# Weights of a macaron block laid out tile by tile by the host, with larger loads and retuned block numbers

## The chip, the core and the metric

The kernel runs on one core of a Trainium2 chip. TensorE (PE) multiplies, VectorE (DVE) and ScalarE (ACT) work element by element, GpSimd (POOL) does small things, and SyncE (SP) issues most DMA transfers. The metric is the device time of one execution in microseconds (us); given is the median of the runs.

## The reference

One transformer block for 256 tokens of width 2048, in float32: a SwiGLU FFN (hidden width 5632), a mixer (an RWKV-7 scan beside a pooling branch), and a second FFN, each with norms around it.

```python
def _swiglu(x, w_gate, w_up, w_down):
    return (jax.nn.silu(x @ w_gate) * (x @ w_up)) @ w_down

def _hybrid_mixer(u, w_in, ...):
    p = u @ w_in
    z_a, z_b, g_a, g_b = jnp.split(p, IN_SPLITS, axis=-1)
    y_a = _rwkv7_branch(z_a, ...) @ w_proj_a
    y_b = _pool_branch(z_b, pool_w, pool_scale) @ w_proj_b
    m = jax.nn.sigmoid(g_a) * y_a + jax.nn.sigmoid(g_b) * y_b
    return m @ w_out
...
        f = _swiglu(_rmsnorm(h, ln_ffn1_pre[l]), ffn1_gate[l], ffn1_up[l], ffn1_down[l])
        h = h + MACARON_WEIGHT * _rmsnorm(f, ln_ffn1_post[l])
        mx = _hybrid_mixer(_rmsnorm(h, ln_mix_pre[l]), ...)
        h = h + _rmsnorm(mx, ln_mix_post[l])
        f = _swiglu(_rmsnorm(h, ln_ffn2_pre[l]), ffn2_gate[l], ffn2_up[l], ffn2_down[l])
        h = h + MACARON_WEIGHT * _rmsnorm(f, ln_ffn2_post[l])
```

## The kernel before

**Products.** The 256 tokens are two row halves (h = 0, 1) of 128. A weight matrix is cut into tiles of 128 rows (index k) by 512 columns. Every float32 value is kept as a high and a low half: ACT casts a loaded weight (w) to its high half (wH), DVE subtracts it and leaves the low half (wL); the activations have xH and xL. One product is one row half times one tile, three matmuls of 512 columns (`mm3`: high x high, high x low, low x high). Weight tiles come two at a time (1024 columns wide) by `get_w` into one of 5 buffers w and are split into one of 5 pairs wH, wL. All these loads are issued on SP. In the old layout a load reads rows of 512 floats, 2 KB, out of the matrix as it is given.

**Quads.** For a pair of k tiles and two column blocks f and l (gate and up in the gate/up part, two column blocks of the down or output weights) there are 2 x 2 x 2 = 8 products. A quad does them in 7, with sums of weight tiles and sums of activation tiles. `raw4` loads its four weight tiles (into va and vb), DVE makes the sums (t13, then a sum written into w, then t4), and `halves` splits them. In the gate/up part a quad is done in two pieces: `early` (4 products), in the block before its own, and `late` (3 products, with the other two tiles loaded again by its own load) in its own block. `quad` does all seven at once in the down part and in the mixer's output.

**Order of the gate/up part.** There are 11 blocks of 512 gate columns and 512 up columns, each 16 k tiles deep. GATE1 and GATE2 give the number of quads of each block in the first and the second FFN. `block_seq` lays out a block's pieces: plain pairs of the gate, the late parts of its own quads between them, plain pairs of the up weights, and, spread over all of these, the early parts of the next block's quads. After each block DVE transposes the activations, and they go out to DRAM and back (cx, x).

**Parts' begins and ends.** The first product set of the first FFN (`head`) takes tokens from x_t, loaded a k tile or two at a time between the weights (xT), and k tiles one after the other. In the mixer and the second FFN the first set goes through `by_half`: the first LEAD k tiles are multiplied with row half 0, then with row half 1, so that row half 1 may be normalized later. There, the tiles from number STAG on get halves in buffers of their own (kH, kL, out of 34 units "u"). The same function does the last TRAIL tiles of a part's down product.

**Who sets the order.** The code records every operation (`Plan.add`), and a planner (`simulate`) works out an order for each engine with a list scheduler: it has a price for each operation (`cost`; for a DMA, bytes by a rate), a due time (`deadlines`), and a count of free buffers, and among ready operations it takes the one that is due first. The matmuls keep their program order within three streams: the scan chain first, then transposes ("side"), then the rest ("main"). `can` refuses an operation whose buffer isn't free; its rule on units keeps the last one for the scan chain. The result is emitted by one loop, so that all operations have the line L494 in the profile, and tiles are told apart by name. `set(behind=..., lag=...)` sets an operation's predecessor or due time; in `head` the sum of squares for the first norm (xq, px) starts behind k tile 11. `normed` forms the normalized activations (nx) and their sums (sf) for the quads.

## Time and profile before

| what | before |
|---|---|
| median of 3 runs | 2003.32 us (2002.46 to 2004.37) |
| the profiled execution | 2001.42 us, its span 1999.6 us |
| PE busy | 1988.3 us |
| DVE busy | 1782.8 us |
| ACT busy | 1179.8 us |
| loads issued on SP: bytes of that queue, share of the 16 DMA engines' time | 466.11 MB, 73.9% |

The span is the time from the first to the last instruction of the profiled execution. An engine's share says how much of it the engine was busy; a stage is read from its own stretch of the time. "[0.57 <-DVE wL]" behind a row means that the engine was idle for 0.57 us before it and that DVE's write of wL ended that. "512.0 KB, 4.7" in a row on transfers is the size of one and the median us from issue to landing. Names drop their numbers: f and l are the two column blocks' sums in PSUM, mm those of plain sets, p the extra sums of a quad, hH and hL the halves of t4.

### The profile page before, as it was taken

To read this page: it belongs to the slowest core of one execution; us is meant where nothing else is said; L and a number is where in the kernel's file an instruction comes from. 1 tells how busy PE (TensorE), PEld (TensorE's weight loads), DVE (VectorE), ACT (ScalarE), POOL (GpSimd) and SP (SyncE) were. 2 spreads that over 40 slices of the span, in tenths; PEclk is the share of its full clock that TensorE was granted. 3 is DMA by queue.
4 is the path that set the end of the run, shared out by engine and by line. 5 is a ranking of instruction groups with operands and counts; after the bars stand their busy time and mean duration, and the time that the engine had idled before them with its cause. 6 is when DMAs were issued, how large, how long until landed. Compare 5 with 4: busy or idle time off the path is not lost.

```text
span 1999.6 us, 28096 instructions
## 1 busy us (share of the span) xinstructions
PE 1988.3 (99%) x9751; PEld 1641.3 (82%) x9751; DVE 1782.8 (89%) x2320; ACT 1179.8 (59%) x1557; POOL 75.4 (4%) x142
## 2 busy tenths in 40 slices
PE   9999999999999999999999999999999999999998
PEld 7888888888888888888888788888888888788886
DVE  8989999999989867898859879898999999998896
ACT  7555556566555656864646445575555655655563
POOL 0000000000000020002200100010000000000000
PEclk9999999999999999999999999999999999999999
DMA  8788888887667787767576567777888888976674
GB/s 282 237 261 267 279 264 283 267 283 229 219 197 255 235 261 233 216 194 244 151 218 183 177 202 228 259 233 244 266 278 262 272 282 274 281 225 212 200 253 147
DMA packets 263198, 477.47 MB, mean 239 GB/s; under 512 B 22928, under 2 KB 50832, under 8 KB 263056
## 3 DMA queue, kind: packets, MB, share of 16 engines
q1 hardware_dynamic: 259536, 466.11, 73.9%
q0 software_dynamic: 3232, 9.44, 1.4%
q8 instruction: 76, 1.25, 0.2%
q14 instruction: 66, 0.54, 0.1%
q10 hardware_dynamic: 288, 0.14, 0.0%
HBM read 447.94 MB, written 26.61 MB: 237 GB/s over the span
## 4 chain that ended last, share of the span: by engine, by line
PE 66%; DVE 15%; DMA 9%; issue 7%; ACT 2%; SPq 1%; POOL 0%; DVEq 0%; ACTq 0%; POOLq 0%
PE mm L494 25%; PE l L494 17%; PE f L494 15%; DVE wL L494 7%; DMA w<-in_ffn_gate_dram 6%; PE p L494 5%; DVE t L494 3%; DMA w<-in_ffn_up_dram 2%; ACT wH L494 2%; DVE w L494 1%; SPq L494 1%; DMA x<-cx 1%; DVE sg L494 1%; DVE hL L494 1%; DVE f L494 1%
## 5 line engine op out<-in xcount | busy, mean ns | idle before, releaser
L494 ACT CAST wH<-w 128x1024 fp32r<-128x1024 f32 (+2 forms) x720 | 745.3, 1043 | 627.7 <-PE mm L494 155.6
L494 DVE TENSOR_TENSOR wL<-w,wH 128x1024 fp32r<-128x1024 f32 (+2 forms) x720 | 860.0, 1206 | 135.0 <-ACT wH L494 130.7
L494 PE MATMUL l<-wL,xH 128*128 128x512 f32 x770 | 300.0, 390 | 0.0
L494 PE MATMUL l<-wH,xL 128*128 128x512 f32 x770 | 299.6, 389 | 0.0
L494 PE MATMUL l<-wH,xH 128*128 128x512 f32 x770 | 299.6, 389 | 0.0
L494 PE MATMUL mm<-wL,xH 128*128 128x512 f32 (+1 forms) x656 | 254.6, 388 | 1.1 <-DVE wL L494 1.0
L494 PE MATMUL mm<-wH,xH 128*128 128x512 f32 (+1 forms) x656 | 254.3, 388 | 0.3 <-ACT xH L494 0.3
L494 PE MATMUL mm<-wH,xL 128*128 128x512 f32 (+1 forms) x656 | 253.8, 387 | 0.0
L494 PE MATMUL f<-wL,xH 128*128 128x512 f32 x644 | 251.0, 390 | 0.4 <-DVE wL L494 0.3
L494 PE MATMUL f<-wH,xH 128*128 128x512 f32 x644 | 250.7, 389 | 0.0
L494 PE MATMUL f<-wH,xL 128*128 128x512 f32 x644 | 250.5, 389 | 0.0
L494 DVE TENSOR_TENSOR t<-w,w 128x1024 f32<-128x1024 f32 (+1 forms) x166 | 168.9, 1017 | 18.4 <-DMA w<-in_ffn_gate_dram 14.1
L494 PEld LDWEIGHTS l<-wL,xH 128*128 128x128 f32 x770 | 144.5, 188 | 31.5 <-DVE wL L494 1.5
L494 PEld LDWEIGHTS l<-wH,xL 128*128 128x128 f32 x770 | 144.6, 188 | 29.8
L494 PEld LDWEIGHTS l<-wH,xH 128*128 128x128 f32 x770 | 144.6, 188 | 29.8
L494 PEld LDWEIGHTS mm<-wL,xH 128*128 128x128 f32 x656 | 123.2, 188 | 26.4 <-DVE wL L494 2.4
L494 PEld LDWEIGHTS mm<-wH,xH 128*128 128x128 f32 x656 | 123.2, 188 | 25.1 <-ACT xH L494 0.7
L494 PEld LDWEIGHTS mm<-wH,xL 128*128 128x128 f32 x656 | 123.2, 188 | 24.3 <-DVE xL L494 0.2
L494 PEld LDWEIGHTS f<-wL,xH 128*128 128x128 f32 x644 | 120.9, 188 | 26.6 <-DVE wL L494 1.7
L494 PEld LDWEIGHTS f<-wH,xL 128*128 128x128 f32 x644 | 120.9, 188 | 25.2
L494 PEld LDWEIGHTS f<-wH,xH 128*128 128x128 f32 x644 | 120.9, 188 | 24.9
L494 DVE TENSOR_TENSOR wL<-t,wH 128x1024 fp32r<-128x1024 f32 x103 | 125.2, 1216 | 3.9 <-ACT wH L494 3.6
(310 smaller groups left out, 2778.8 us busy)
## 6 DMA issues: line engine op xcount, KB each, us to landing
w<-in_w_in_dram SPq DMA_DIRECT2D x128, 512.0 KB, 4.5
w<-in_ffn_up_dram SPq DMA_DIRECT2D x113, 512.0 KB, 4.7
w<-in_ffn_gate_dram SPq DMA_DIRECT2D x109, 512.0 KB, 4.8
w<-in_ffn_down_dram SPq DMA_DIRECT2D x104, 512.0 KB, 4.5
w<-in_ffn_gate_dram SPq DMA_DIRECT2D x197, 256.0 KB, 4.2
w<-in_ffn_up_dram SPq DMA_DIRECT2D x189, 256.0 KB, 4.2
w<-in_ffn_down_dram SPq DMA_DIRECT2D x144, 256.0 KB, 3.9
cx<-T SPq DMA_DIRECT2D x32, 512.0 KB, 3.6
```

What stands on the lines that cost most here:

```text
L494: ins = o.fn(*[real(x) for x in o.a], **{n: real(x) for n, x in o.k.items()})
```

## The change

The host lays the large weights out. For gate with up, for down and for w_out (`Pairs`), the four tiles of a k pair and of the two column blocks stand side by side, 2048 floats a partition: plain pairs as f0, f1, l0, l1; quads as l0, f1, l1, f0, so that va and vb are each one piece of 4 KB a partition and the late part's two tiles (f1, l1) another. For w_in and the two projections (`Blocks`) a k pair of a column block is one piece of 1024 floats a partition. The narrow w_l and pool_w (`Rows`) and the tokens x_t stand k tile beside k tile, one long row a partition. `get_w` and `raw4` read these pieces; a quad's first part has two loads instead of four, a late part one instead of two.

The tokens of the first part are loaded at k = 1, 2, 4, 8 and 12, in pieces of 1, 2, 4, 4 and 4 k tiles. LEAD is 16 and STAG 6: at a part's begin all 16 k tiles go by row halves, and those from number 6 on have units of their own. GATE1 and GATE2 change at two and one places. In `ffn` the gate's activations are recorded ahead of the up product set and the squares' end (`finish`: px and the root) after the gate's. The planner's price of a load follows the longer runs (RATE), CARRY is longer, and a second rule on units (SPARE2) holds back operations of the scan chain that lie ahead of its next matmul while four or fewer units are free.

On SP at the kernel's start the loads stand so in the kernel before (w are weights, xT tokens):

```order
L494 DMA w_37_133<-in_ffn_gate_dram 128x512
L494 DMA xT_131<-in_x_t_dram 128x256
L494 DMA w_38_144<-in_ffn_gate_dram 128x512
L494 DMA xT_131<-in_x_t_dram 128x256
L494 DMA w_39_153<-in_ffn_gate_dram 128x512
L494 DMA xT_131<-in_x_t_dram 128x256
L494 DMA w_40_160<-in_ffn_gate_dram 128x512
L494 DMA xT_162<-in_x_t_dram 128x256
L494 DMA w_41_166<-in_ffn_gate_dram 128x512
```

and so in the changed one:

```order
L552 DMA w_37_133<-in_gate_up_dram 128x512
L552 DMA xT_131<-in_x_t_dram 128x256
L552 DMA w_38_144<-in_gate_up_dram 128x512
L552 DMA xT_131<-in_x_t_dram 128x512
L552 DMA w_39_153<-in_gate_up_dram 128x512
L552 DMA w_40_158<-in_gate_up_dram 128x512
L552 DMA xT_161<-in_x_t_dram 128x1024
L552 DMA w_41_163<-in_gate_up_dram 128x512
```

The tokens of k tiles 4 to 7 (128x1024) now stand ahead of the weight tile of k = 4.

On DVE, where the gate's product set of the first FFN ends and the up weights begin (wL_406 of before and wL_357 after are the first low half of the up weights, nx and xq the norm's adds), before:

```order
L494 TENSOR_TENSOR wL_361<-w_48_265,wH_352 128x1024
L494 TENSOR_TENSOR nx_370<-xH_168,xL_176 128x1024
L494 TENSOR_TENSOR xq_363<-xq_363,xq_372 128x1024
L494 TENSOR_TENSOR nx_389<-xH_215,xL_227 128x1024
L494 TENSOR_TENSOR xq_378<-xq_378,xq_385 128x1024
L494 TENSOR_TENSOR wL_406<-w_84_276,wH_393 128x1024
```

and after:

```order
L552 TENSOR_TENSOR wL_350<-w_48_237,wH_338 128x1024
L552 TENSOR_TENSOR wL_357<-w_84_247,wH_348 128x1024
L552 TENSOR_TENSOR nx_368<-xH_169,xL_178 128x1024
L552 TENSOR_TENSOR wL_379<-w_87_257,wH_359 128x1024
L552 TENSOR_TENSOR xq_366<-xq_366,xq_376 128x1024
L552 TENSOR_TENSOR nx_398<-xH_222,xL_227 128x1024
```

The first low half of the up weights moved from behind four adds to ahead of them.

On SP, where the first quad of the first FFN is loaded (w_161 and w_162 are its va and vb, cx the activations of block 0 on their way to DRAM), before:

```order
L494 DMA w_158_605<-in_ffn_gate_dram 128x2x512
L494 DMA w_161_626<-in_ffn_up_dram 128x512
L494 DMA w_161_626<-in_ffn_gate_dram 128x512
L494 DMA cx_87<-T_108_635 128x1024
L494 DMA w_162_655<-in_ffn_gate_dram 128x512
L494 DMA w_162_655<-in_ffn_up_dram 128x512
```

and after:

```order
L552 DMA w_158_591<-in_gate_up_dram 128x1024
L552 DMA cx_87<-T_108_620 128x1024
L552 DMA w_161_641<-in_gate_up_dram 128x1024
L552 DMA w_162_649<-in_gate_up_dram 128x1024
```

Four loads became two, and the store to cx stands ahead of both.

The diff, cut to its core:

```diff
@@ -36,8 +36,8 @@
-STAG = 8
-LEAD = 12
+STAG = 6
+LEAD = 16
@@ -47,13 +47,14 @@
-GATE1 = [0, 0, 2, 4, 3, 4, 3, 4, 3, 4, 4]
-GATE2 = [0, 0, 3, 4, 3, 4, 3, 4, 3, 4, 4]
+GATE1 = [0, 0, 2, 4, 3, 4, 3, 4, 3, 4, 3]
+GATE2 = [0, 0, 4, 4, 3, 4, 3, 4, 3, 4, 3]
+SPARE2 = 4
@@ -65,7 +66,60 @@
+XLOADS = {1: 1, 2: 2, 4: 4, 8: 4, 12: 4}
+SQLAG = 4000.0
+def down_quads(plan):
+    return [[2 * i for i in range(nq)] for nq, _, _ in plan]
+class Pairs:
+    def __init__(s, ap, KT, where):
+        s.ap, s.KT, s.where = ap, KT, where
+    def row(s, r):
+        return s.ap[r * P:r * P + P]
+    def get(s, j, n, c0, cw):
+        b, side = s.where(c0 // 512)
+        o = side * 1024 + j % 2 * 512
+        return s.row(b * s.KT // 2 + j // 2)[:, o:o + n * 512]
+    def quad(s, k, c0):
+        return s.row(s.where(c0 // 512)[0] * s.KT // 2 + k // 2)
+class Blocks:
+    def __init__(s, ap, KT, cols):
+        s.ap, s.KT, s.cols = ap, KT, cols
+    def get(s, j, n, c0, cw):
+        r = s.cols.index(c0) * s.KT // 2 + j // 2
+        return s.ap[r * P:r * P + P, j % 2 * 512:j % 2 * 512 + n * 512]
+class Rows:
+    def __init__(s, ap):
+        s.ap = ap
+    def get(s, j, n, c0, cw):
+        return s.ap[:, j * cw:(j + n) * cw]
+IN_COLS = ([z * W + h * 512 for z in range(3) for h in range(2)]
+           + [RCOLS + b * 512 for b in range(2)]
+           + [g + c * 512 for g in (GA, GB) for c in range(4)])
+ALL_COLS = [c * 512 for c in range(4)]
@@ -89,9 +143,10 @@
+RATE = 410.0
-CARRY = 1800.0
+CARRY = 2000.0
@@ -219,9 +274,8 @@
-            run = min(min(y.shape[-1] for y in w + r) * 4, 2048)
-            o.dur = o.nbytes / (387.0 if run >= 2048 else 387.0 * max(run, 64) * 1.25
-                                / (run + 512))
+            run = min(min(y.shape[-1] for y in w + r) * 4, 4096)
+            o.dur = o.nbytes / min(RATE, 484.0 * max(run, 64) / (run + 512))
@@ -320,9 +374,13 @@
-                if i.tag == "u" and o.stream != "chain" and len(slots["u"]) <= SPARE:
+                if i.tag == "u" and len(slots["u"]) <= max(SPARE, SPARE2):
-                    if q and q[0].nom <= o.nom < q[0].nom + HOLD:
+                    few = len(slots["u"]) <= SPARE
+                    if q and o.stream != "chain" and few and q[0].nom <= o.nom < q[0].nom + HOLD:
+                        return False
+                    if q and o.stream == "chain" and len(slots["u"]) <= SPARE2 \
+                            and o.nom > q[0].nom:
@@ -580,9 +638,7 @@
-        s.nc.sync.dma_start(out=w32[:, :n * cw].rearrange("p (k c) -> p k c", k=n),
-                            in_=w[j * P:(j + n) * P, c0:c0 + cw]
-                            .rearrange("(k p) c -> p k c", p=P))
+        s.nc.sync.dma_start(out=w32[:, :n * cw], in_=w.get(j, n, c0, cw))
@@ -711,8 +767,8 @@
         k = 0
         first(load, None, None)
         while k < KT:
-            if k:
-                first(load, k, n(k))
+            if k in XLOADS:
+                first(load, k, XLOADS[k])
             first(get, k, n(k))
             k += n(k)
         for k in range(4):
@@ -802,12 +858,11 @@
         s.nc.scalar.activation(out=s.rtmp("junk").bitcast(mybir.dt.bfloat16), in_=src,
                                func=AF.Square, accum_out=acc)
 
-    def raw4(s, k, wf, cf, wl, cl):
-        va, vb = [s.raw().rearrange("p (a c) -> p a c", a=2) for _ in range(2)]
-        for dst, kk, w, c0 in ((va[:, 0], k, wl, cl), (vb[:, 0], k, wf, cf),
-                               (va[:, 1], k + 1, wf, cf), (vb[:, 1], k + 1, wl, cl)):
-            s.nc.sync.dma_start(out=dst, in_=w[kk * P:kk * P + P, c0:c0 + 512])
-        return va, vb
+    def raw4(s, k, w, c0):
+        v = [s.raw() for _ in range(2)]
+        for i in range(2):
+            s.nc.sync.dma_start(out=v[i], in_=w.quad(k, c0)[:, i * 1024:i * 1024 + 1024])
+        return [t.rearrange("p (a c) -> p a c", a=2) for t in v]
 
     def halves(s, v, tag=None):
         m = v.shape[1]
@@ -874,10 +929,9 @@
-        vc = q.raw().rearrange("p (a c) -> p a c", a=2)
-        for i, (w, c0) in enumerate(((s.wf, s.cf), (s.wl, s.cl))):
-            q.nc.sync.dma_start(out=vc[:, i], in_=w[k * P + P:k * P + 2 * P, c0:c0 + 512])
-        b22, b21 = q.halves(vc)
+        vc = q.raw()
+        q.nc.sync.dma_start(out=vc, in_=s.wf.quad(k, s.cf)[:, 512:1536])
+        b22, b21 = q.halves(vc.rearrange("p (a c) -> p a c", a=2))
@@ -898,16 +952,16 @@
-        va, vb = q.raw4(k, s.wf, s.cf, s.wl, s.cl)
+        va, vb = q.raw4(k, s.wf, s.cf)
-        V.tensor_tensor(out=t13, in0=va, in1=vb[:, :1].to_broadcast([P, 2, 512]),
+        V.tensor_tensor(out=t13, in0=va, in1=vb[:, 1:].to_broadcast([P, 2, 512]),
-        V.tensor_tensor(out=vb[:, 0], in0=va[:, 0], in1=t13[:, 1], op=ALU.add)
+        V.tensor_tensor(out=vb[:, 1], in0=va[:, 0], in1=t13[:, 1], op=ALU.add)
-        V.tensor_tensor(out=t4, in0=vb[:, 1], in1=vb[:, 0], op=ALU.subtract)
+        V.tensor_tensor(out=t4, in0=vb[:, 0], in1=vb[:, 1], op=ALU.subtract)
-        t2, b21 = q.halves(vb)
+        b21, t2 = q.halves(vb)
@@ -1000,9 +1054,13 @@
         pss = [], []
 
         def hold(i):
-            return lambda h, ps: (pss[i].append(ps), h and ev("fl"[i], pss[i]))
+            return lambda h, ps: pss[i].append(ps)
         s.gemm_tok(wg, 0, at, NKD, hold(0), lead=True, xs=xs)
+        if xs:
+            xs[3]()
+        ev("f", pss[0])
         s.gemm_tok(wu, 0, at, NKD, hold(1))
+        ev("l", pss[1])
         rb = s.rtmp("rsb")
         s.spread(rs, rb)
         su = []
@@ -1874,15 +1936,15 @@
-                nc.scalar.dma_start(out=xT[0][:, :1], in_=x_t[:P].unsqueeze(1))
+                nc.scalar.dma_start(out=xT[0][:, 0], in_=x_t[:, :S])
-                out=xT[k // 4][:, k % 4:k % 4 + n],
-                in_=x_t[k * P:(k + n) * P].rearrange("(k p) t -> p k t", p=P))
+                out=xT[k // 4].rearrange("p k t -> p (k t)")[:, k % 4 * S:(k % 4 + n) * S],
+                in_=x_t[:, k * S:(k + n) * S])
...
+    def pairs(blocks, quads):
+        out = []
+        for (f, l), q in zip(blocks, quads):
+            kt = len(f)
+            v = _np.empty((kt // 2, P, 4, 512), _np.float32)
+            for i in range(kt // 2):
+                f0, f1, l0, l1 = f[2 * i], f[2 * i + 1], l[2 * i], l[2 * i + 1]
+                for m, t in enumerate((l0, f1, l1, f0) if 2 * i in q else (f0, f1, l0, l1)):
+                    v[i, :, m] = t
+            out.append(v.reshape(-1, 4 * 512))
+        return _np.concatenate(out)
+    def blocks(a, cols):
+        return _np.concatenate([tiles(a, c).reshape(-1, 2, P, 512).transpose(0, 2, 1, 3)
+                                .reshape(-1, 1024) for c in cols])
...
```

More of the change, by code (lines that the diff above doesn't have):

```diff
@@ L729, in head @@
                 s.late = last
-                with s.set(behind=last, lag=4000.0):
+                with s.set(behind=last, lag=SQLAG):
                     square()
@@ L1050, in down @@
     def down(s, wd, at, KT, ev, hT, sm, plan):
[L1051 to L1053 removed]
+        for c, (nq, first, step), ks in zip((0, 2), plan, down_quads(plan)):
+            J = Columns(s, wd, c * 512, wd, c * 512 + 512, at, KT, sm, ks, s.bank, s.psum)
             quads = list(J.quads)
@@ L1892, in turn @@
                                            op0=ALU.mult, op1=ALU.subtract)
+        sq = []
         def squares():
@@ L1966, in laid_out @@
         o += n * P
-    return (("x_t", _np.ascontiguousarray(_np.asarray(inputs["x"])[0].T)),
-            ("cols", _np.ascontiguousarray(cols.reshape(NCOL, P).T)))
+    return (("x_t", _np.ascontiguousarray(rows(_np.asarray(inputs["x"])[0].T, 0, S))),
+            ("cols", _np.ascontiguousarray(cols.reshape(NCOL, P).T)),
+            *((n, _np.ascontiguousarray(v, _np.float32)) for n, v in big))
 def kernel(**inputs):
```

74 lines of the change are left out of this document (50 added, 24 removed).

## The prediction

> **What bounds the kernel now.** I read the page first, then the stretches of the span by engine, then the waits of TensorE (PE) alone, and last the places in time where PE stops.
>
> ```profile
> span 1999.6 us, 28096 instructions
> PE 1988.3 (99%) x9751; PEld 1641.3 (82%) x9751; DVE 1782.8 (89%) x2320; ACT 1179.8 (59%) x1557; POOL 75.4 (4%) x142
> ```
> ```profile
> 150.00:420.00 270.00, 270.00 (x1192) 223.28 (x1190) 254.93 (x285) 160.45 (x195) 0.00 (x0) 1.00 0.85 273
> 740.00:900.00 160.00, 159.73 (x858) 135.71 (x857) 135.09 (x243) 108.08 (x181) 6.91 (x9) 1.00 0.72 217
> 900.00:1210.00 310.00, 309.81 (x2188) 252.82 (x2187) 253.10 (x443) 164.00 (x235) 35.77 (x57) 1.00 0.66 198
> 1300.00:1345.00 45.00, 45.00 (x209) 37.25 (x209) 44.10 (x79) 34.31 (x69) 8.36 (x10) 1.00 0.75 231
> ```
> ```profile
> PE po L494 <- ACT dg L494: 2.1, 1, 2.1
> ...
> PE mm L494 <- DVE wL L494: 1.0, 2, 0.6
> PE f L494 <- DVE wL L494: 0.9, 3, 0.6
> ```
> The columns of the stretches are length, then busy time (and count) of PE, weight load, DVE, ACT and POOL, granted clock, DMA share, GB/s. PE is busy throughout at the full clock, with 1192 matmuls in 270.00 us, so one matmul of 512 columns costs 0.2265 us and one product (three of them) 0.68 us. Its waits on weights add up to 1.9 us, and one wait of 2.1 us is in the last output. So what a faster DMA can buy directly is small. DVE is next: 254.93 of 270 us in the gate/up stretch, with DMA at 0.85. The real price of each stop is read from start to start:
>
> ```profile
> 17.01 0.39 PE L494 MATMUL mm<-wH,xH 128*128 128x512 f32 x1
> 17.97 0.50 PE L494 MATMUL mm<-wL,xH 128*128 128x512 f32 x1 [0.57 <-DVE wL L494]
> ...
> 28.75 0.39 PE L494 MATMUL mm<-wH,xH 128*128 128x512 f32 x1
> 29.59 0.50 PE L494 MATMUL mm<-wL,xH 128*128 128x512 f32 x1 [0.44 <-DVE wL L494]
> ...
> 420.63 0.40 PE L494 MATMUL f<-wH,xH 128*128 128x512 f32 x1
> 421.18 0.50 PE L494 MATMUL f<-wL,xH 128*128 128x512 f32 x1 [0.15 <-DVE wL L494]
> ...
> 1712.05 0.40 PE L494 MATMUL f<-wH,sH 128*128 128x512 f32 x1
> 1713.02 0.50 PE L494 MATMUL f<-wL,sH 128*128 128x512 f32 x1 [0.56 <-DVE wL L494]
> ...
> 1716.45 0.40 PE L494 MATMUL f<-wH,xH 128*128 128x512 f32 x1
> 1717.02 0.50 PE L494 MATMUL f<-wL,xH 128*128 128x512 f32 x1 [0.17 <-DVE wL L494]
> ```
> Less the 0.23 us that a matmul takes anyway, these stops cost 0.73, 0.61, 0.32, 0.74 and 0.34 us: 2.74 us, each a wait for a low half of a weight from DVE.
>
> **Term 1, the products.** GATE1 sums to 30 quads in place of 31; GATE2 stays at 32, one quad moving from the last block to block 2. A quad does 7 products where plain tiles do 8. One quad fewer is 3 matmuls more: 3 x 0.2265 = +0.68 us, all on PE, nothing hides it.
>
> **Term 2, the start.**
> ```profile
> 14.13 0.91 ACT L494 ACTIVATE xH<-xT,cols 128x256 fp32r<-128x256 f32 x2 [0.50 <-DMA xT<-in_x_t_dram]
> 15.61 1.05 ACT L494 CAST wH<-w 128x1024 fp32r<-128x1024 f32 x1 [0.56 <-DVE xL L494]
> ```
> ```profile
> 23.77 1.22 DVE L494 TENSOR_TENSOR nx<-xH,xL 128x1024 f32<-128x1024 f32 x1
> ...
> 28.31 1.22 DVE L494 TENSOR_TENSOR wL<-w,wH 128x1024 fp32r<-128x1024 f32 x1
> ```
> On SP the tokens now come in 5 loads instead of 11, four k tiles (512 KB) at a time, ahead of the weights that need them; queued behind them are the weight tiles of k = 4, 8 and 12. On ACT the cast of weight tiles 8 and 9 stands behind four token tiles instead of two: 0.91 us more work in front, from the row at 14.13. The gain is fewer and longer pieces, and the wait of 0.50 us there may go. So the stop at 17.01 may grow by up to 0.9 or vanish (-0.73). I take +0.3, nearer the ACT row, since the work there is certain. The stop at 28.75 is different: DVE did four adds of 1024 columns (23.77 to 28.31) ahead of the first low half of the up weights. Now that half comes first, the next ones are mixed among the adds, and the stop of 0.61 goes. What is late next is the sum of squares and with it the first gate's activations, which PE does not wait for while it multiplies the up weights. Net -0.3, ends -1.34 and +0.9.
>
> **Term 3, the gate/up blocks.** One early quad and its late part on DVE, from block 2 of the second FFN:
> ```profile
> 1415.96 1.23 DVE L494 TENSOR_TENSOR t<-w,w 128x1024 f32<-128x1024 f32 x1 [0.98 <-DMA w<-in_ffn_gate_dram]
> ...
> 1418.31 0.69 DVE L494 TENSOR_TENSOR w<-w,t 128x512 f32<-128x512 f32 x1
> 1419.03 0.69 DVE L494 TENSOR_TENSOR t<-w,w 128x512 f32<-128x512 f32 x1
> 1419.64 0.68 DVE L494 TENSOR_TENSOR hL<-t,hH 128x512 fp32r<-128x512 f32 x1
> 1420.24 1.22 DVE L494 TENSOR_TENSOR wL<-w,wH 128x1024 fp32r<-128x1024 f32 x1
> 1421.38 1.22 DVE L494 TENSOR_TENSOR wL<-t,wH 128x1024 fp32r<-128x1024 f32 x1
> ```
> ```profile
> 1422.17 0.39 PE L494 MATMUL l<-wL,xH 128*128 128x512 f32 x1
> ```
> Early: 1.23 + 0.69 + 0.69 + 1.22 + 1.22 = 5.05 us; late: 1.22 + 0.68 = 1.90; a plain pair of tiles of one column 1.22. PE takes 4 products early, 3 late, 4 for a plain pair. With q quads finished and n begun a block has 64 - 5q + 4n products and 2(8 - q) plain splits. Four and four (before: block 9 alone): DVE 8 x 1.22 + 4 x 1.90 + 4 x 5.05 = 37.6 us under PE's 60 x 0.68 = 40.8, to which the sums, activations and transposes at the block's end are added. Three and four: 38.1 under 44.2. Four and three: 32.5 under 38.1. So DVE's spare is 3.2, 6.1 and 5.6 us, and it is the four-and-four block where PE stops. The FFNs begin here:
> ```profile
> 5.39 0.51 PE L494 MATMUL mm<-wH,xH 128*128 128x512 f32 x1 [0.27 <-ACT xH L494]
> ...
> 1302.68 0.39 PE L494 MATMUL mm<-wH,xH 128*128 128x512 f32 x1
> ```
> Blocks 0 to 8 hold 569 products in the first and 568 in the second, 387 and 386 us, so block 9 runs from about 392 to 433 and from about 1689 to 1730 us: the stops at 420.63, 1712.05 and 1716.45 are all in it. Now block 9 is four and three: these 0.32 + 0.74 + 0.34 = 1.40 us go. In the first FFN no new four-and-four block appears. In the second, block 2 becomes one: its spare falls by 2.9 us. Its lead is thin: the low half begun at 1420.24 ends at 1421.46 and is used at 1422.17, 0.71 us later. So up to 2.9 - 0.71 = 2.2 us of new stops, or none. Measured stops of such a block are 0.32 and 1.08 us. I take 0.3, the lower one, since block 2 has full buffers at its start and DVE's waits for data there (0.98 us in the row above) should shorten.
>
> **Term 4, the transfers.**
> ```profile
> w<-in_ffn_up_dram SPq DMA_DIRECT2D x113, 512.0 KB, 4.7
> w<-in_ffn_gate_dram SPq DMA_DIRECT2D x109, 512.0 KB, 4.8
> w<-in_ffn_down_dram SPq DMA_DIRECT2D x104, 512.0 KB, 4.5
> w<-in_ffn_gate_dram SPq DMA_DIRECT2D x197, 256.0 KB, 4.2
> ...
> cx<-T SPq DMA_DIRECT2D x32, 512.0 KB, 3.6
> ```
> A quad's four loads of 256 KB become two of 512 KB and the late pair becomes one; plain pairs stay 512 KB but one piece of 4 KB a partition instead of two of 2 KB. The nearest row with 4 KB rows is the store to cx, 3.6 us against 4.7 for weights; it is the other direction, so I put a load between 3.6 and 4.8. PE hides all of it except the stops already counted, so the term is 0. If that cover were gone (DVE late), it is term 3's range. On SP 276 issues fall away; they bring nothing by themselves, since what SP waits for is buffers that DVE gives back:
> ```profile
> SPq L494 <- DVE wL L494: 913.6, 547, 12.3
> ```
>
> A rule speaks against the layout. The new weight rows lie 4 or 8 KB apart. In the old layout those of ffn_down do too (2048 floats), and their 512 KB land in 4.5 us, against 4.8 for ffn_gate, whose rows are 22.5 KB apart: no loss at that pitch. The Trainium skill, "DMA: Bandwidth & Descriptors", section "Latency and other measured facts", reports copies slowed by rows a large power of two apart (207 GB/s at 512 KiB, 103 at 4 MiB) and advises laying tiles out contiguously. By that rule carried down to 8 KB the sum would be the fourth rival's below; the trace disagrees at 8 KB, and by the row the term stays 0.
>
> **Term 5, the parts' begins and the mixer.** Sixteen k tiles by row halves ask for 8 splits, 8 x 1.22 = 9.8 us of DVE, within 16 x 3 x 0.2265 = 10.9 us, before it was 6 in 8.2. PE has no idle time at 1300 to 1345, so nothing can be won; DVE is busy 44.10 of 45, so one split (1.22) may come late, but five pairs now have buffers of their own and can be made before. I take 0, ends 0 and +1.2. In the mixer the planner's new rule on free units moves the second scan chain's pieces; PE idles 0.27 + 0.19 us there, so -0.5 is the one end, and the other, by the longest wait PE has anywhere, +2.1. I take 0. The last output's wait of 2.1 us stays.
>
> **Sum.** +0.68 - 0.3 - 1.40 + 0.3 = -0.72 us on the profiled execution's 2001.42 (span 1999.6 and 1.8 around it). The median of the runs, 2003.32, lies 1.9 above that; I keep the difference and predict 2002.6 us.
>
> **Rivals.** First, data waits matter more than this execution shows: all 2.74 us of stops go, block 2 gets none, and the 1.9 us between profile and median are waits for DMA too. Then 2003.32 - 2.74 - 1.9 + 0.68 = 1999.4, and with the mixer's 0.5 it is 1998.9. For it: DMA shares of 0.85. Against it: PE's own waits are so few that it needs every one of them.
>
> Second, the other side: the first subtraction of an early quad reads both of its 512 KB tiles, so it waits for the later of two long loads instead of four short ones. 62 early quads stand in the two FFNs. With four early quads and 3.2 to 6.1 us of spare in a block, less what the blocks' ends take, a quad may be about 1 us later before DVE becomes the bound. The rows speak against it: 512 KB land 0.6 us later than 256 KB, and there are two issues fewer ahead. It decides from 1 us on; at 1.1 it costs 62 x 0.1 = 6 us, 2009.5, at 1.3 it is 2022.
>
> Third, the transfers do not get faster and block 2 stops for its 2.2 us: the sum is +0.68 - 0.3 - 1.40 + 2.2 = +1.2, 2004.5, still the same time.
>
> Fourth, rows a power of two apart slow the loads by a third: stretches with a DMA share of 0.85 would need 0.85 x 1.33 = 1.13 of their time, +0.13 on some 780 us of gate/up work, about +100 us.
>
> **How the numbers follow.** The time of a run is known to about 0.2%, 4 us, and this is the bound of "same". The forecast has 0.55, the third rival 0.07: same 0.62. The first rival has 0.20, faster. The second has 0.15 and the fourth 0.03: slower 0.18. From the values taken, the low ends lie 1.04 + 0.3 + 0.5 us below (terms 2, 3 and 5), and the high ends 1.2, 1.9, 1.2 and 2.1 above; with all low ends or the two largest high ones at once the forecast's own range is 2000.8 to 2006.6. To take in the first rival, with 2 us for the spread of the runs, and the mild part of the second I give 1997 to 2009.5.
>
> **What would show it.** The count of 512-column matmuls up by 3; no stop near 420 and 1712; stops, if any, near 1420 and around 18; the first up weight's low half ahead of nx on DVE; the DMA share in the gate/up stretch below 0.85 at the same GB/s. A PE wait of over a microsecond in any FFN block, or DVE waiting for w in most quads, would make the prediction wrong.

## The result, and the profile after

| | before | after |
|---|---|---|
| median of 5 runs each | 2004.37 us (2002.46 to 2005.14) | 2052.44 us (2045.79 to 2057.76) |
| the profiled execution | 2001.42 us | 2045.79 us |

The change makes the kernel slower: ratio 1.0234, 95% interval 1.0207 to 1.0261. The forecast was 2002.6 us with 2009.5 as its upper end; the time lies 43 us above that end.

The span, the busy times and four stretches of the changed kernel (the columns are those of the stretches before; the times are the same, so that the last three stretches begin some 20 to 25 us earlier in the work than they did before):

```profile
span 2044.1 us, 27486 instructions
PE 2003.3 (98%) x9754; PEld 1645.0 (80%) x9754; DVE 1782.9 (87%) x2315; ACT 1176.5 (58%) x1555; POOL 74.1 (4%) x142
```
```profile
150.00:420.00 270.00, 259.47 (x1122) 212.03 (x1121) 242.87 (x270) 152.40 (x185) 0.00 (x0) 0.99 0.80 259
740.00:900.00 160.00, 159.67 (x820) 135.79 (x819) 123.18 (x213) 102.30 (x164) 9.72 (x16) 1.00 0.74 222
900.00:1210.00 310.00, 307.44 (x2208) 249.88 (x2208) 253.17 (x454) 165.99 (x249) 35.92 (x57) 1.00 0.59 187
1300.00:1345.00 45.00, 44.47 (x209) 36.49 (x208) 42.61 (x79) 35.37 (x74) 7.99 (x12) 1.00 0.78 260
```

The loss is in the FFNs. The mixer's first product begins at 716.56 us (before 696.13), the second FFN's at 1327.49 (1302.68): the first FFN costs 20.4 us, the mixer 4.4 and the rest 19.7. In the gate/up stretch PE begins 1122 matmuls in the 270 us in which it began 1192. DMA moves less there (259 GB/s, before 273) at a lower share, and DVE does less too. Each is less busy than before, so none of them has become the bound. PE's own waits, and those of DVE for weights (columns: total us, times, longest us), first after and then before:

```profile
PE l L552 <- DVE hL L552: 15.6, 8, 3.3
PE l L552 <- DVE wL L552: 3.5, 4, 1.2
PE l L552 <- ACT hH L552: 2.7, 3, 1.5
...
DVE t L552 <- DMA w<-in_gate_up_dram: 32.9, 25, 3.8
```
```profile
DVE t L494 <- DMA w<-in_ffn_gate_dram: 14.1, 16, 1.6
DVE t L494 <- DMA w<-in_ffn_up_dram: 2.3, 2, 1.4
```

DVE's t, the first subtraction of a quad, waited 16.4 us for weights and now waits 32.9, at longest 3.8 us. PE, which had no wait in an FFN block over 0.6 us, now waits 15.6 us in eight places for hL, the low half of a quad's t4. The largest of these, seen on PE, on DVE and on ACT:

```profile
171.70 0.39 PE L552 MATMUL l<-hH,xH 128*128 128x512 f32 x1
175.34 0.61 PE L552 MATMUL l<-hL,xH 128*128 128x512 f32 x1 [3.26 <-DVE hL L552]
175.76 0.63 PE L552 MATMUL l<-hH,xL 128*128 128x512 f32 x1
176.18 0.63 PE L552 MATMUL f<-wH,xH 128*128 128x512 f32 x1
```
```profile
169.13 1.23 DVE L552 TENSOR_TENSOR wL<-w,wH 128x1024 fp32r<-128x1024 f32 x1 [1.55 <-ACT wH L552]
171.87 1.29 DVE L552 TENSOR_TENSOR xL<-x,xH 128x512 fp32r<-128x512 f32 x2 [1.51 <-ACT xH L552]
173.46 1.23 DVE L552 TENSOR_TENSOR t<-w,w 128x1024 f32<-128x1024 f32 x1 [0.30 <-DMA w<-in_gate_up_dram]
174.60 0.69 DVE L552 TENSOR_TENSOR hL<-t,hH 128x512 fp32r<-128x512 f32 x1
```
```profile
169.00 0.61 ACT L552 CAST hH<-t 128x512 fp32r<-128x512 f32 x1
171.21 1.14 ACT L552 CAST xH<-x 128x512 fp32r<-128x512 f32 x2 [1.60 <-DMA x<-cx]
```

The hL that PE needed at 171.93 asks DVE for 0.69 us of work on a t4 made in the block before and on an hH that ACT ended at 169.61. But it stands in DVE's fixed order behind a split of activations (which waited 1.51 us for ACT, which waited for a transfer from cx) and behind the t of the next block's quad (which waited for its weights). So late transfers stop PE through work that PE doesn't need yet. After the stop the matmuls follow 0.42 us apart and last 0.6 us: the clock is granted at half. From start to start, 159 gaps of 512-column matmuls longer by over 0.05 us than the usual 0.2265 add up to 50.6 us, the last output left out (before 113 of 13.9), and 32 matmuls at half clock add 6.4. With 0.7 for the three matmuls more that is 43.8 of the 44.5 us between the two spans.

The transfers (columns: issues, KB each, median us to landing):

```profile
w<-in_gate_up_dram SPq DMA_DIRECT2D x410, 512.0 KB, 5.4
w<-in_down_dram SPq DMA_DIRECT2D x176, 512.0 KB, 4.6
```

The gate and up loads, which landed in 4.8 and 4.7 us (256 KB in 4.2), land in 5.4.

### The profile page after: what moved, and what is told of

Same layout as the page of the kernel before. It is cut to its first block, busy times and chain, and to the rows that moved or that the text cites. A ratio compares the mean times of both kernels' runs of the same rounds, so it can differ in the third digit from the quotient of the medians.

```text
span 2044.1 us, 27486 instructions
## 1 busy us (share of the span) xinstructions
PE 2003.3 (98%) x9754; PEld 1645.0 (80%) x9754; DVE 1782.9 (87%) x2315; ACT 1176.5 (58%) x1555; POOL 74.1 (4%) x142
## 5 line engine op out<-in xcount | busy, mean ns | idle before, releaser
L552 ACT CAST wH<-w 128x1024 fp32r<-128x1024 f32 (+1 forms) x711 | 734.2, 1042 | 661.8 <-DVE w L552 176.0
L552 DVE TENSOR_TENSOR wL<-w,wH 128x1024 fp32r<-128x1024 f32 (+1 forms) x711 | 850.1, 1208 | 164.1 <-ACT wH L552 159.9
L552 PE MATMUL mm<-wH,xL 128*128 128x512 f32 (+1 forms) x632 | 245.7, 389 | 0.0
L552 PE MATMUL mm<-wH,xH 128*128 128x512 f32 (+1 forms) x632 | 244.9, 387 | 0.7 <-ACT xH L552 0.5
L552 PE MATMUL mm<-wL,xH 128*128 128x512 f32 (+1 forms) x632 | 244.1, 386 | 1.0 <-DVE wL L552 1.0
L552 DVE TENSOR_TENSOR t<-w,w 128x1024 f32<-128x1024 f32 (+1 forms) x164 | 167.4, 1021 | 35.7 <-DMA w<-in_gate_up_dram 32.9
L552 PEld LDWEIGHTS mm<-wL,xH 128*128 128x128 f32 x632 | 118.7, 188 | 25.2 <-DVE wL L552 2.2
L552 PEld LDWEIGHTS mm<-wH,xH 128*128 128x128 f32 x632 | 118.7, 188 | 24.6 <-ACT wH L552 1.1
L552 PEld LDWEIGHTS mm<-wH,xL 128*128 128x128 f32 x632 | 118.6, 188 | 23.8 <-DVE xL L552 0.2
```

Source lines behind the costliest of these rows:

```text
L552: ins = o.fn(*[real(x) for x in o.a], **{n: real(x) for n, x in o.k.items()})
```

## The experiments

Ratios are against the kernel before, timed beside each set of runs (2004.2 to 2004.7 us), with 95% intervals.

**First round: price, numbers, load size.** Three theories were put up after the traces. A: the planner now believes loads to be faster (410 against 387 bytes/ns), and so puts work on DVE and ACT ahead of data that isn't there. B: a quad's 512 KB loads land later. C: the new block numbers and rules.

e1_old_price, the changed kernel with the planner's old price:
```diff
-            run = min(min(y.shape[-1] for y in w + r) * 4, 4096)
-            o.dur = o.nbytes / min(RATE, 484.0 * max(run, 64) / (run + 512))
+            run = min(min(y.shape[-1] for y in w + r) * 4, 2048)
+            o.dur = o.nbytes / (387.0 if run >= 2048 else 387.0 * max(run, 64) * 1.25
+                                / (run + 512))
-CARRY = 2000.0
+CARRY = 1800.0
```


> The changed kernel with the planner's old price of a load (387 bytes a ns for runs of 2 KB and more, CARRY 1800); layout, load sizes, block numbers as changed. Theory A (the planner, with the higher rate, orders DVE and ACT for data that land later than it thinks, so PE waits for low halves that stand behind a wait for data): under 2015 us, and PE's waits for hL (15.6 us in the changed kernel) under 5 us. Theory B (loads of 512 KB for the quads land later than four of 256 KB): 2035 us or more. Theory C (the block numbers, LEAD, STAG and SPARE2): 2035 us or more.

Measured 2033.62 us (2030.21 to 2043.28), ratio 1.0152 [1.0124, 1.0180]: 18.8 us less than the changed kernel, between the two theories. DVE's waits for gate_up fell to 21.3 us, PE's for hL only to 12.6, where theory A had under 5.

e2_old_tuning, the changed kernel with the old numbers:
```diff
-STAG = 6
-LEAD = 16
+STAG = 8
+LEAD = 12
-GATE1 = [0, 0, 2, 4, 3, 4, 3, 4, 3, 4, 3]
-GATE2 = [0, 0, 4, 4, 3, 4, 3, 4, 3, 4, 3]
+GATE1 = [0, 0, 2, 4, 3, 4, 3, 4, 3, 4, 4]
+GATE2 = [0, 0, 3, 4, 3, 4, 3, 4, 3, 4, 4]
-SPARE2 = 4
+SPARE2 = 0
```


> The changed kernel with STAG 8, LEAD 12, the old GATE1 and GATE2 and no second rule on units; layout, load sizes and price as changed. Theory C: under 2015 us. Theories A and B: 2035 us or more, with stops of 1 to 3 us in the gate/up blocks as before this edit.

Measured 2046.85 us (2043.13 to 2050.76), ratio 1.0210 [1.0189, 1.0232]. The interval overlaps that of the changed kernel; the numbers are not the cause of the 48 us.

e3_small_loads, quads loaded in 256 KB pieces from the new layout (early parts four loads, late parts two):
```diff
-            s.nc.sync.dma_start(out=v[i], in_=w.quad(k, c0)[:, i * 1024:i * 1024 + 1024])
+            for j in range(2):
+                o = i * 1024 + j * 512
+                s.nc.sync.dma_start(out=v[i][:, j * 512:j * 512 + 512],
+                                    in_=w.quad(k, c0)[:, o:o + 512])
...
-        q.nc.sync.dma_start(out=vc, in_=s.wf.quad(k, s.cf)[:, 512:1536])
+        for j in range(2):
+            q.nc.sync.dma_start(out=vc[:, j * 512:j * 512 + 512],
+                                in_=s.wf.quad(k, s.cf)[:, 512 + j * 512:1024 + j * 512])
```


> The changed kernel with a quad's first part loaded as four pieces of 256 KB and its late part as two, from the new layout (runs of 2 KB); all else as changed. Theory B: under 2015 us. Theories A and C: 2035 us or more.

Measured 2033.01 us (2028.53 to 2035.01), ratio 1.0138 [1.0118, 1.0157]: 19.4 us less, again between the theories, 2 us below what A and C foresaw.

e4_new_price_on_before, the kernel before with the new price for its 2 KB pieces:
```diff
-            o.dur = o.nbytes / (387.0 if run >= 2048 else 387.0 * max(run, 64) * 1.25
+            o.dur = o.nbytes / (410.0 if run >= 2048 else 387.0 * max(run, 64) * 1.25
-CARRY = 1800.0
+CARRY = 2000.0
```


> The kernel before with the planner's price of a load at 410 bytes a ns and CARRY 2000; nothing else. Theory A: slower than before by 10 us or more, with PE waits for hL. Theories B and C: within 4 us of before.

Measured 2011.78 us (2009.61 to 2013.75), ratio 1.0034 [1.0021, 1.0047]. The price alone costs the old kernel some 7 us, between the expectations. No one theory of the three held; A and B each had a part.

**Second round: what is left when the order is that of before.**

e5_old_price_small_loads, the edits of e1 and e3 together:
```diff
+            o.dur = o.nbytes / (387.0 if run >= 2048 else 387.0 * max(run, 64) * 1.25
...
+                s.nc.sync.dma_start(out=v[i][:, j * 512:j * 512 + 512],
```


> The changed kernel with the old planner price and with a quad's pieces loaded 256 KB at a time; the new block numbers stay. Theory D (price and load size are two separate causes that add, 19 us each): 2008 to 2018 us. If both runs took away the same loss: 2028 to 2036. Theory E (what is left is the new layout or the new block numbers): not below 2018.

Measured 2022.98 us (2017.64 to 2025.39), ratio 1.0095 [1.0078, 1.0112]: above what adding causes would leave. Something else was there.

e6_only_the_layout, the edits of e1, e2 and e3 together. DVE's and ACT's orders then are those of before but for under one per cent of their rows; what is left is the layout, the tokens' loads and the steps moved in `ffn`:
```diff
+STAG = 8
+LEAD = 12
+GATE2 = [0, 0, 3, 4, 3, 4, 3, 4, 3, 4, 4]
...
+            o.dur = o.nbytes / (387.0 if run >= 2048 else 387.0 * max(run, 64) * 1.25
...
+                s.nc.sync.dma_start(out=v[i][:, j * 512:j * 512 + 512],
```


> Old price, 256 KB pieces for quads, old block numbers, LEAD, STAG and no rule of four units: DVE and ACT then stand in almost the order of before, and what is left of the change is the host's layout with its 4 KB pieces for plain pairs, and the tokens' loads. Theory D: 2000 to 2008 us. Theory E, the layout's half: 2015 or more. Theory E, the block numbers' half: within 4 us of before while the run with the new block numbers stays 10 us above this one.

Measured 2021.83 us (2018.92 to 2023.74), ratio 1.0084 [1.0069, 1.0099]. The order is that of before, and the kernel is 17 us slower. Its loads, by the layout alone, and DVE's wait:

```profile
w<-in_gate_up_dram SPq DMA_DIRECT2D x222, 512.0 KB, 5.2
w<-in_gate_up_dram SPq DMA_DIRECT2D x386, 256.0 KB, 4.8
w<-in_down_dram SPq DMA_DIRECT2D x104, 512.0 KB, 4.5
w<-in_down_dram SPq DMA_DIRECT2D x144, 256.0 KB, 3.9
...
DVE t L553 <- DMA w<-in_gate_up_dram: 28.8, 26, 2.2
```

The 256 KB loads of gate_up take 0.6 us more than those of before, though they have the same number of pieces of the same 2 KB. Only where the pieces lie is different.

e7_layout_2k_pieces, as e6 with a plain pair's tiles put as f0, l0, f1, l1, so that its load reads 2 KB pieces:
```diff
-            for m, t in enumerate((l0, f1, l1, f0) if 2 * i in q else (f0, f1, l0, l1)):
+            for m, t in enumerate((l0, f1, l1, f0) if 2 * i in q else (f0, l0, f1, l1)):
```


> As the run before, but the host puts a plain pair's tiles in the order f0, l0, f1, l1, so that a plain pair's load reads pieces of 2 KB again, 4 KB apart from each other. If 4 KB pieces are what slows the loads: 5 us or more under the run before. If the size of a piece does not matter (the theory of the trace): within 3 us of it.

Measured 2018.22 us (2015.58 to 2021.80), ratio 1.0069 [1.0054, 1.0084]; 3.6 us below e6, between the two expectations, and the intervals overlap. The size of a piece is not what costs the 17 us.

e8_pessimistic_price, the changed kernel with a lower price than the old one:
```diff
-RATE = 410.0
+RATE = 350.0
-CARRY = 2000.0
+CARRY = 4000.0
```


> The changed kernel with a planner price below the old one (RATE 350, CARRY 4000) and nothing else changed. Theory A (the planner puts work on DVE and ACT ahead of data that is not there yet): lower than with the old price, 2010 to 2028 us, with DVE's waits for the weights below 21 us. Theory B (512 KB loads of a quad are late whatever the order): 2030 or more.

Measured 2041.12 us (2040.49 to 2041.98), ratio 1.0182 [1.0167, 1.0197], DVE's waits for gate_up 31.4 us: theory A in its simple form missed. A planner that thinks loads slower than they are does not make a better order either.

**Third round: the distance between rows.** In the new layout a load's 128 rows lie 8192 bytes apart (Pairs: 2048 floats a row). Theory F: this distance slows the loads.

e9_pitch_8448, as e6 with rows padded to 2112 floats:
```diff
-            v = _np.empty((kt // 2, P, 4, 512), _np.float32)
+            v = _np.zeros((kt // 2, P, 2112), _np.float32)
...
-                    v[i, :, m] = t
+                    v[i, :, m * 512:m * 512 + 512] = t
-            out.append(v.reshape(-1, 4 * 512))
+            out.append(v.reshape(-1, 2112))
...
-        return s.ap[r * P:r * P + P]
+        return s.ap[r * P:r * P + P, :2048]
```


> As the run with only the layout, but the rows of gate_up, down and w_out are padded from 2048 to 2112 floats, so that the partitions of a load stand 8448 bytes apart and not 8192. Theory F (the power-of-two distance between a load's rows slows it while other loads run): back to 2000 to 2009 us, and the 512 KB loads of gate_up land in 4.7 to 4.9 us, not 5.2. Theory G (something else of the layout: the two weights in one tensor, the place in memory, the tokens' loads): within 4 us of the unpadded one, 2018 to 2026.

Measured 2004.27 us (2000.54 to 2006.96), ratio 1.0002 [0.9992, 1.0011]: all 17 us are gone; the 512 KB loads land a little sooner than expected. The rows that answer to those of e6:

```profile
w<-in_gate_up_dram SPq DMA_DIRECT2D x222, 512.0 KB, 4.6
w<-in_gate_up_dram SPq DMA_DIRECT2D x386, 256.0 KB, 4.2
w<-in_down_dram SPq DMA_DIRECT2D x104, 512.0 KB, 3.9
w<-in_down_dram SPq DMA_DIRECT2D x144, 256.0 KB, 3.5
...
DVE t L553 <- DMA w<-in_gate_up_dram: 12.4, 18, 1.4
```

Both programs have the same instructions in the same order; 256 bytes between rows take 0.6 us from the median gate_up load and 0.4 to 0.6 from the down loads.

e10_pitch_22528, as e9 with 5632 in place of 2112:
```diff
-            out.append(v.reshape(-1, 4 * 512))
+            out.append(v.reshape(-1, 5632))
```


> As the run before, with rows of 5632 floats, 22528 bytes, the distance that the gate and up weights have in the layout of before. Theory F: 2000 to 2009 us. If a load's rows should stand close together whatever their distance: no better than the run with 8448 bytes. Theory G: 2018 to 2026.

Measured 2003.37 us (1999.11 to 2006.38), ratio 0.9993 [0.9984, 1.0002]. The distance of the old layout is as good; closeness doesn't matter.

e11_change_pitch_8448, the changed kernel with the padding of e9 and nothing else:
```diff
-            out.append(v.reshape(-1, 4 * 512))
+            out.append(v.reshape(-1, 2112))
```


> The changed kernel with nothing but the rows padded to 8448 bytes. Theory F: 14 to 20 us below the changed kernel, 2030 to 2038 us, price and 512 KB loads still costing the rest. If the pitch is behind all three losses (the price and the large loads only hurt because the loads were slow): below 2012. Theory G: 2045 or more.

Measured 2019.96 us (2018.54 to 2021.42), ratio 1.0078 [1.0063, 1.0093]. Padding takes 32.5 of the 48 us; I had expected less.

**Fourth round: the other 16 us, with good rows.**

e12_pitch_and_price, e11 with the old price of e1:
```diff
-CARRY = 2000.0
+CARRY = 1800.0
...
+            out.append(v.reshape(-1, 2112))
```


> The changed kernel with rows of 8448 bytes and the old planner price. If the price still costs its 19 us with a good pitch: 2001 to 2005 us. If most of that loss came through the slow loads: 2010 to 2018.

Measured 2007.76 us (2004.71 to 2012.71), ratio 1.0015 [1.0004, 1.0025]: 12.2 us less than e11, between the two expectations.

e13_pitch_price_numbers, e12 with the old numbers of e2:
```diff
-GATE2 = [0, 0, 4, 4, 3, 4, 3, 4, 3, 4, 3]
+GATE2 = [0, 0, 3, 4, 3, 4, 3, 4, 3, 4, 4]
...
+            out.append(v.reshape(-1, 2112))
```


> Rows of 8448 bytes, old price, old block numbers; of the change only the 512 KB loads of quads, the layout and the tokens' loads are left. Against the run of 2004.27 us with 256 KB loads this is the size of a quad's loads alone. Theory B (a quad's large loads land later and DVE waits): 2010 to 2020 us. If they only hurt with slow loads: 2000 to 2007.

Measured 2016.13 us (2013.91 to 2018.18), ratio 1.0057 [1.0042, 1.0073], as theory B had it: 11.9 us more than e9, from which it differs in the size of the quads' loads and in the order that the planner then makes. DVE waits for gate_up 13.6 us in all in the profiled run, hardly more than e9's 12.4, but for 3.1 us at the longest and not 1.4. That such long single waits are the cause isn't shown: e15 below has one of 2.7 us and loses nothing.

```profile
DVE t L553 <- DMA w<-in_gate_up_dram: 13.6, 11, 3.1
...
w<-in_gate_up_dram SPq DMA_DIRECT2D x411, 512.0 KB, 4.8
```

e14_dense_tiles, as e6 with each pair of tiles as one contiguous block:
```diff
-            out.append(v.reshape(-1, 4 * 512))
+            out.append(v.reshape(kt // 2, P, 2, 1024).transpose(0, 2, 1, 3).reshape(-1, 1024))
...
-        return s.ap[r * P:r * P + P]
+        return s.ap[2 * r * P:2 * r * P + 2 * P].rearrange("(z p) c -> p z c", z=2)
```


> As the run with only the layout (old price, 256 KB loads for quads, old block numbers), but a pair of tiles is one contiguous block of 128 rows of 4 KB, so rows stand 4096 bytes apart with nothing between. If any power of two as a distance hurts: 2015 us or more. If only the gaps hurt (a load that touches every second 4 KB): 2000 to 2008.

Measured 2004.48 us (2002.64 to 2006.96), ratio 0.9999 [0.9989, 1.0009]. Rows 4096 bytes apart, a power of two too, cost nothing where no gap lies between them.

e15_pitch_price_small, e5 with the padding of e9:
```diff
-CARRY = 2000.0
+CARRY = 1800.0
...
+                s.nc.sync.dma_start(out=v[i][:, j * 512:j * 512 + 512],
...
+            out.append(v.reshape(-1, 2112))
```


> Rows of 8448 bytes, old price, 256 KB loads for quads; the new block numbers, LEAD, STAG and the rule of four units stay. Against 2004.27 us this is the new numbers alone. If they do what they are said to: 2001 to 2006 us (3 matmuls more, the stops of block 9 gone). If they cost DVE its lead: 2008 or more.

Measured 2004.45 us (2000.86 to 2006.73), ratio 1.0002 [0.9993, 1.0012]. The new numbers cost nothing with small loads; with large ones they are worth 8.4 us (e12 against e13). DVE's waits for gate_up are 7.6 us here, 2.7 at the longest.

e16_change_dense, the changed kernel with the blocks of e14:
```diff
-                s.nc.sync.dma_start(out=v[i], in_=w.quad(k, c0)[:, i * 1024:i * 1024 + 1024])
+                s.nc.sync.dma_start(out=v[i], in_=w.quad(k, c0)[:, i])
...
+            q.nc.sync.dma_start(out=vc[:, j * 512:j * 512 + 512],
+                                in_=s.wf.quad(k, s.cf)[:, j, 512 - j * 512:1024 - j * 512])
```


> The changed kernel with each 512 KB piece as one contiguous block, 4096 bytes from row to row (a late part's load takes two pieces of 2 KB out of two blocks), nothing else changed. If gaps alone slowed the loads: like the padded one, 2016 to 2024 us. If the late parts' shorter pieces matter: 2024 to 2032.

Measured 2018.76 us (2016.92 to 2022.47), ratio 1.0073 [1.0058, 1.0088]: as the padded one (e11).

e17_pitch_and_small, e3 with the padding of e9:
```diff
+                s.nc.sync.dma_start(out=v[i][:, j * 512:j * 512 + 512],
...
+            out.append(v.reshape(-1, 2112))
```


> The changed kernel with rows of 8448 bytes and 256 KB loads for quads; the new price stays, which for the 2 KB pieces of these loads is 387 as before and for 4 KB pieces 410. If the price and the load size share one loss (a 512 KB load comes later than the planner thinks): 2004 to 2010 us. If they add: 2013 or more.

Measured 2010.93 us (2006.09 to 2014.06), ratio 1.0025 [1.0011, 1.0038], between the two expectations.

**The three causes side by side**, medians in us, all with the new block numbers:

| rows apart | a quad's loads | new price | old price |
|---|---|---|---|
| 8192 bytes | 512 KB | 2052.4 (after) | 2033.6 (e1) |
| 8192 bytes | 256 KB | 2033.0 (e3) | 2023.0 (e5) |
| 8448 bytes | 512 KB | 2020.0 (e11) | 2007.8 (e12) |
| 8448 bytes | 256 KB | 2010.9 (e17) | 2004.5 (e15) |

Down a column from the upper pair to the lower one, the distance of the rows is worth 18.5 to 32.5 us. The price is worth 6.5 to 18.8 (with 256 KB loads the new price differs for the plain pairs' loads and in CARRY alone), the size of the loads 3.3 to 19.4. Each costs most where the others are bad too, as it would if all three used up the same spare time of DVE and ACT ahead of PE; that reading was not tested by itself. No version is faster than before by more than the 0.2% that can be told; the best, e10, is at 0.9993 with an interval that holds 1.

**How the distance slows a load.** The packet records of e6 and e9 show a 4 KB packet taking 200.6 and 200.7 ns on average, so a packet is not slower. What differs is how many packets are under way at once. Counted from the packet records, from 150 to 420 us (gate and up weights) and from 500 to 680 us (mostly down weights):

```
kernel       rows apart  mean packets   share of time with  share of time with
                         under way      16 or more          8 to 12
150 to 420 us
before       22528       13.65          0.50                0.14
after        8192        12.75          0.39                0.21
e6           8192        13.18          0.37                0.21
e9           8448        13.52          0.46                0.15
e14          contiguous  13.39          0.48                0.17
500 to 680 us
before       8192        11.17          0.21                0.32
e6           8192        11.04          0.20                0.26
e9           8448        11.30          0.34                0.16
e14          contiguous  11.51          0.40                0.19
```

In the first stretch the changed kernel and e6 also stop PE, which delays later loads, so that fewer packets could be an effect of the loss. In the second PE never stops, and e6 and e9 do the same work:

```profile
500.00:680.00 180.00, 180.00 (x796) 149.10 (x795) 166.01 (x186) 104.65 (x116) 3.55 (x24) 1.00 0.69 225
500.00:680.00 180.00, 180.00 (x796) 149.05 (x795) 165.01 (x186) 104.98 (x118) 3.55 (x24) 1.00 0.71 227
```

There too the times with 16 or more packets are rarer with rows 8192 bytes apart. That would fit engines that finish their part of a load at different times; but up to 24 packets are under way at once, so the count isn't one of engines, and the records don't name the engine of a packet: the reason stays open.

## Why the prediction was wrong, point by point

**The step that failed** is in term 4: "no loss at that pitch". It rested on the old down weights, which have rows 8 KB apart and land in 4.5 us, against 4.8 for the gate's at 22.5 KB. That compared two different stretches. The gate loads run in one with a DMA share of 0.85; most of the down loads of the first FFN in this one:

```profile
500.00:680.00 180.00, 180.00 (x796) 149.09 (x795) 166.21 (x187) 105.03 (x118) 3.55 (x24) 1.00 0.70 228
```

There less traffic stands in the way, and 4.5 us was already the slowed value: with padded rows these loads take 3.9 (e9), and those of 256 KB, which read 2 KB pieces in both kernels, 3.5 for 3.9. The packets under way from 500 to 680 us agree: before is like e6, not like e9. The row of 4.5 us could not show that distance doesn't matter; it needed one with the same traffic and another distance, and there was none. The Trainium skill's rule ("DMA: Bandwidth & Descriptors", section "Latency and other measured facts"), which was set aside for this row, points the right way: its two remedies, padding the rows and laying tiles out contiguously, each take back the whole 17 us (e9, e14). Its figures begin at rows 512 KiB apart, and for rows 4 MiB apart it has 4 KiB of padding as a help and 192 bytes as none; here rows 8 KiB apart already cost, and 256 bytes of padding were enough. The landing that term 4 put between 3.6 and 4.8 us was 5.4.

**"PE hides all of it except the stops already counted"** failed with it, and the term that was put at 0 is worth 17 us at the order of before: there loads land 0.6 us later (e6 against e9). The prediction said DVE's spare in a block was 3.2 to 6.1 us and let that stand as cover; but DVE and ACT take their work in a fixed order, so that a late load holds up also what doesn't need it, and a block's spare doesn't help a matmul that is due now.

**A term was missing: the price.** The new planner price was described in front of the prediction and costed at nothing. With good rows it costs 12.2 us with 512 KB loads and 6.5 with 256 KB, and about 7 on the kernel before (e4).

**The second rival** (a quad's 512 KB loads land later) had a true cause. With good rows these loads take 4.8 us in e13 against 4.2 for 256 KB in e9, which is the 0.6 of the prediction, and at the old price they cost 3.3 us with the new numbers and 11.9 with the old; its threshold of 1 us was too high. **The fourth rival** had the main cause and the wrong size: it took a third off the rate and 100 us, with a chance of 0.03. The rate of a packet didn't change at all; the landing did, and the cost was 17 us at the order of before and 32 in the changed kernel.

**Term 1** was right: 9754 matmuls for 9751.

**Term 2** came out inside its ends, with the other sign. The stop at 28.75 is gone, since the first low half of the up weights now comes ahead of the adds. The one at 17.01 (0.73 us) grew to 1.03, by the 0.3 that was taken, but one ahead of it, 0.30 before, grew too:

```profile
9.12 0.50 PE L552 MATMUL mm<-wH,xH 128*128 128x512 f32 x1
9.85 0.50 PE L552 MATMUL mm<-wL,xH 128*128 128x512 f32 x1 [0.23 <-DVE wL L552]
...
18.24 0.50 PE L552 MATMUL mm<-wH,xH 128*128 128x512 f32 x1
19.50 0.50 PE L552 MATMUL mm<-wL,xH 128*128 128x512 f32 x1 [0.76 <-DVE wL L552]
```

Less a matmul each, all stops of over 0.2 us in the first 40 us cost 2.3 us, for 1.6 before: +0.6 in place of -0.3. That the stop at 17.01 grew by just the 0.3 that was taken was in part luck: in e15, whose loads come in time, the same tokens stand ahead of the same cast on ACT, the stop is 0.17 us and all of them cost 0.9. One at 65.67 of 0.27 us became 0.85, in e9 and e15 too; no term had it.

**Term 3** can't be read in the changed kernel, whose stops of 1 to 3.4 us drown it, but in e15, which has the new numbers and loads in time. (GATE1 in fact changes at one place and GATE2 at two.) No stop of over 0.3 us is left near 420, 1712 or 1716. e9 with the old numbers has the two late ones, 1.16 us in all, but not the one at 420, so that the new numbers aren't what took that away. Near 1420, where 0.3 us was foreseen, stands one of 0.33 us; one of 0.98 wasn't foreseen and lies, by 0.68 us a product, in block 6, a three-and-four block with 6.1 us of spare in the prediction:

```profile
1427.62 0.39 PE L553 MATMUL f<-wH,xH 128*128 128x512 f32 x1
1428.17 0.50 PE L553 MATMUL f<-wL,xH 128*128 128x512 f32 x1 [0.17 <-DVE wL L553]
```
```profile
1588.00 0.45 PE L553 MATMUL l<-wH,xH 128*128 128x512 f32 x1
1589.21 0.50 PE L553 MATMUL l<-wL,xH 128*128 128x512 f32 x1 [0.76 <-DVE wL L553]
```

So the stops of block 9 went as foreseen, but the new ones cost as much, and the time stays the same with small loads (e15 against e9). The 8.4 us with large loads were not foreseen.

**Term 5** was right at the second FFN's begin and wrong for the mixer. The second FFN begins at 1327.49 us in the changed kernel, and PE stops nowhere there:

```profile
1327.00:1372.00 45.00, 45.00 (x206) 37.15 (x205) 44.37 (x73) 31.08 (x56) 6.29 (x9) 1.00 0.62 203
```

From the mixer's first product to there 606.6 us became 610.9: 4.4 us more, where +2.1 was the end. The second rule on units is not the cause by itself: e15 keeps it and takes 607.5. The mixer wasn't taken apart by runs of its own.

**What would show it** named both signs that came: a PE wait of over a microsecond in an FFN block, and DVE waiting for weights (in 25 quads, not most). The DMA share in the gate/up stretch fell below 0.85, as it was to, but the GB/s fell with it, from 273 to 259.

## What to carry to other kernels

Before a load is given a new layout, look at how far apart its rows lie: 2 or 4 KB used out of every 8 KB made loads land 0.6 us later, and 256 bytes of padding or contiguous blocks took that back. Other powers of two with gaps were not tried. A landing time may be compared only between transfers that run in the same traffic; a row from a quieter stretch bounds nothing. Where engines work in an order fixed ahead, spare time summed over a block is no cover for a transfer that comes late, and a planner's belief about transfers is a change to the kernel that wants its own term.

## What was not expected of the hardware

- Pieces twice as long brought hardly any rate: a 2 KB packet took 102.8 ns on average in the kernel before (19.9 bytes/ns) and a 4 KB packet 198.8 after (20.6).
- A distance of 8192 bytes between a load's rows slows its landing (5.2 against 4.6 us) while a packet's own time stays the same; 4096 without gaps, 8448 and 22528 don't.
- Stops of PE can cost more than their length. In the changed kernel the granted clock fell to a half at 175.58, 390.62, 1496.54 and 1581.87 us, for 3.41 us each and 6.83 the last time, which adds the 6.4 us named above. The last three of these moments lie 63, 387 and 412 times 3.413 us after the first, on a fixed grid. In the grid's stretches right ahead of the four, PE was idle for 3.2, 2.9, 2.3 and 2.4 us, counted from start to start beyond 0.227 us a matmul; no other stretch at full clock, the last output left out, reached 2.0. The stop of 2.4 us at 259 and the pair of 0.9 and 2.4 at 1754 to 1757 are each cut in two by a line of the grid and left the clock as it was. The Trainium skill ("TensorE: Matmul & The Clock Gate", section "Part 1: The HAM clock gate (the "warmup" mystery)") tells of a free-running window of about 3.4 us over which activity is watched; the 3.41 us of this trace agree.
